# A hybrid encoder trunk: the order of the first unit's projections and the low-rank one in the second token half

## The chip, the cores and the metric

The kernel runs on one core of a Trainium2 chip. The metric is device time in microseconds, from launch to end, as the median of several runs. Beside it there is one execution with the hardware profiler on, whose trace is read here.

The engines are named as the profile names them: PE is TensorE's matrix multiply and PEld its weight load, DVE is VectorE, ACT is ScalarE, POOL is GpSimd, SP is SyncE, on which nearly all transfers are issued. [...]

## The reference

Two layers over 1024 tokens of width 1024. The change is in layer 0, in front of two groups of heads:

```python
h = rmsnorm(x, norm_mix_g[i])
proj = h @ even_w_in[e]                      # r, k, v of RWKV; q, k, v, gate of DeltaNet
dh = token_shift(h) - h
...
r = r + (token_shift(r) - r) * mu_proj[0]    # and so k, v
xw = h + dh * mu_lora[0]
xa = h + dh * mu_lora[1]
xg = h + dh * mu_lora[2]
w_log = -jax.nn.softplus(-(w0 + jnp.tanh(xw @ w1) @ w2).astype(jnp.float32)) - 0.5
decay = jnp.exp(-jnp.exp(w_log))
a = jax.nn.sigmoid(a0 + (xa @ a1) @ a2)
g = jax.nn.sigmoid(xg @ g1) @ g2
...
y = wkv7_scan(rh, heads(decay), kh, vh, -kk, kk * ah)
```

RWKV-7 has eight heads of 64 with a state that is carried from token to token, DeltaNet four heads of 128 in chunks. Their outputs are joined and projected; a squared-ReLU MLP and a gated embedding follow, and layer 1 has banded attention in place of the two groups.

## The kernel before

Activations lie with the feature on the partitions. Every 32-bit product is made of three: weights and activations are split in a rounded high part and a rest (`split_w`, L276 on ACT and L277 on DVE, for weights; `split_scaled`, L320 on ACT and L321 on DVE, for activations), and `mm3` does high times high, high times low and low times high. A projection of one 128-wide output over 512 tokens is so 24 matmuls of 128x512 into one PSUM bank (tag `dense`, name `dps`; there are two such banks in this layer), and is then scaled by the row norm `self.rs` and written out by a DVE instruction (L640 in `project`, L665 for the first part of the low-rank product). The row norm is made of sums of squares: `row_stats` (matmuls with ones, then a reciprocal root of small DVE instructions, L259 to L264) and `to_rows` (four transposes into a bank, a copy on ACT, L354). Both take their bank from the same two.

Layer 0 runs over 16 units: four RWKV pairs of heads and four DeltaNet heads, by turns, for the first 512 tokens (units 0 to 7), and then the same for the other 512 (8 to 15). Six generators ("lanes") emit the work: `in` makes a unit's projections, `front`, `mid`, `back` and `post` its scan, and one makes the cumulated decays. `run` steps through them by an estimated time: a lane gives a key for which it waits, or a name with a delay from a table. `rwkv_in` waits for `("raw", u - 2, j)` ahead of its projection j: for unit 8, until `front` of unit 6 has read its own. The order in which the lanes emit is only a preference: a planner (`schedule_with_timeline_sim=True`) then lays down the order on each engine, by its own picture of when things are ready and when a buffer is free, so loads are often issued far ahead of where they stand in the text.

Buffers that matter here:
- `wraw`, two of 128x1024: raw weights, two of the four tiles of x for the second half, the low-rank weight as it is loaded (`lraw`), its two scaled versions, and `sb`, the second low-rank product.
- `whi` and `wlo`, two each: the split weights, held until their projection is done.
- `xg` (pool `rx`): x of the current half, scaled and split. It can be written for the second half only behind the last matmul of the first that reads it.
- `gate`, two: the gate projection of a DeltaNet unit, held until `gdn_post` has read it (L1160).

`l0_in` is the lane of projections. At unit 8 it does, in this order: four loads of x, eight splits into `xg`, the low-rank product "la" (`lora(0, ...)`), then `rwkv_in` with three projections j = 1, 0, 2, each with a weight load and a split of its own; then `gdn_scalars` (a projection `wba` and a long chain of small DVE instructions) and the other low-rank product "lg". `lora` loads one weight (L651), makes two scaled versions of it on POOL (L659), splits both, runs two projections and adds the results on POOL (L668). At unit 0 the order is already another one: the first weight tile is loaded ahead of x (`self.w_first`), and the three projections come before la.

POOL also runs the substitution of the 16x16 inverses for `front` (`inverse_start`, L376 to L386), whose data go out and back through DRAM (`scr<-N`, `scr<-Ng` L364; `subb` L368; `z` L388; `Xp` L390), issued on SP.

Of the kernel before, what the change touches and what calls it, by code (L numbers as in the profile page):

```python
# [104 lines left out]
class Trunk:  # L105
# [423 lines left out]
    def l0_in(self, units):  # L529
        nc, a, fr = self.nc, self.a, self.fr  # L530
        self.state = {}
        self.xg = []
        for u, (nm, p, hf) in enumerate(units):
            if u % 8 == 0:


                self.xg, squares = [], []
                if hf == 0:
                    acc = fr.tile([P, HB], F32, tag="rsbc", name="acc", bufs=2)
                    self.w_first = self.load_w(a["w_in"][4])  # L540
                else:

                    x2 = [self.load_x(q, self.pre if q < 2 else self.wp, "ph" if q == 0 else "pl" if q == 1 else "wraw")
                          for q in range(4)]
                for k in range(NK):
                    if hf == 0:
                        xr = self.t2()
                        nc.sync.dma_start(out=xr, in_=a["x"][k, :, 0:HB])
                    else:
                        xr = x2[k // 2][:, k % 2, :]  # L550
                    if k % 2 == 0:
                        xg2 = self.pair(k // 2)
                    xg = xg2[:, k % 2]
                    self.split_scaled(xg, xr, self.vec("mixg", k), slice(0, HB))
                    self.xg.append(xg)
                    if hf == 0:
                        squares.append(lambda k=k, xr=xr: self.square(acc, xr, k == 0))
                for f in squares:
                    f()
                if hf == 0:  # L560
                    self.wa2 = fr.tile([P, 512], F32, tag="wa2", name="wa2")
                    nc.sync.dma_start(out=self.wa2, in_=a["wa2"])
                    self.g2 = self.l0.tile([P, 512], F32, tag="g2", name="g2")
                    nc.sync.dma_start(out=self.g2, in_=a["g2"])
                    self.hv = self.l0.tile([P, 2, 4], F32, tag="hv", name="hv")
                    nc.sync.dma_start(out=self.hv.rearrange("p a b -> p (a b)"),
                                      in_=a["gdnhv"].rearrange("(o c) -> o c", o=1).broadcast_to((P, 8)))
                    self.ea = self.l0.tile([P, 1, 4], F32, tag="ea", name="ea")
                    nc.scalar.activation(self.ea, self.hv[:, 0:1, :], AF.Exp)
                sc = {}  # L570
                if hf == 0:
                    rsc = self.sm.tile([P, 4], F32, tag="rsc", name="rsc")
                    self.rs = fr.tile([P, HB], F32, tag="rsbc", name="rsbc", bufs=2)

                    self.extra = [lambda t=t: self.psm.tile([P, HB], F32, tag=t, name="dps") for t in ("y", "ch", "pm")]
                    self.late, self.plan = [], {2: lambda: self.row_stats([acc], rsc), 3: lambda: self.to_rows(rsc, self.rs)}
                    raws = yield from getattr(self, nm + "_in")(p, hf, u)
                else:
                    self.rs = acc
                self.pst = None  # L580
                sc["lwa"] = yield from self.lora(0, [(0, 64, 0), (64, 128, 1)], "la")
                nc.scalar.activation(sc["lwa"][0:64], sc["lwa"][0:64], AF.Tanh)
            if u:
                raws = yield from getattr(self, nm + "_in")(p, hf, u)
            self.state[u] = (raws, sc)
            self.mark(("in", u), 1.0)
            if u == 6:

                acc = fr.tile([P, HB], F32, tag="rsbc", name="acc", bufs=2)
                for q in range(4):  # L590
                    x2 = self.load_x(q, self.pre, "pl" if q % 2 else "ph")
                    for e in range(2):
                        self.square(acc, x2[:, e], q + e == 0)
            if u == 7:
                rsc = self.sm.tile([P, 4], F32, tag="rsc", name="rsc")
                self.row_stats([acc], rsc)
                yield "l0_in1"
                self.to_rows(rsc, acc)
            if u % 8 == 0:

                yield from self.gdn_scalars(hf, sc)
                gg = yield from self.lora(1, [(0, 128, 2)], "lg")
                nc.scalar.activation(gg, gg, AF.Tanh, scale=0.5)
                nc.vector.tensor_scalar(gg, gg, 0.5, 0.5, op0=ALU.mult, op1=ALU.add)
                sc["lg"] = gg
                self.mark(("lg", hf))

        rsb = lambda: fr.tile([P, HB], F32, tag="rsbc", name="xs", bufs=2)
        pt = [self.pair(k) for k in range(2)]
        sc = [self.pair(q, F32) for q in (2, 3)]  # L610
        sc = [t[:, e] for t in sc for e in range(2)]
        yield from self.ple_proj(0, lambda k, hf: pt[k][:, hf], sc[0], lambda n: sc[1 + n % 3], rsb, self.load_w)
        yield from self.out_early(0, a["x"], self.pair, rsb, self.load_w, [("post", 7), ("post", 13), ("post", 14), ("post", 15)])
# [127 lines left out]
    def rwkv_in(self, p, hf, u):  # L741
        raws = []
        for j in (1, 0, 2):
            if u >= 2:
                yield ("raw", u - 2, j)
            w = self.load_w(self.a["w_in"][4 * j + p]) if u or j != 1 else self.w_first
            raws.append((yield from self.project(w, f"r{p}{j}", 1)))
        return [raws[1], raws[0], raws[2]]

# [1219 lines left out]
```

## Time and profile before

| | us |
|---|---|
| median of 3 runs | 3195.7 |
| lowest and highest run | 3192.25, 3198.93 |
| span of the profiled execution | 3188.9 |
| PE busy | 3080.8 (97%) |
| PEld busy | 2580.6 (81%) |
| DVE busy | 2005.1 (63%) |
| ACT busy | 1405.7 (44%) |
| POOL busy | 531.1 (17%) |

The span reaches from the first to the last instruction of the profiled execution; the median of the runs is 6.8 us above it. Busy time of PE is not work at full speed: the ends of matmuls are modelled, and TensorE's clock can be granted in part, which the profile shows as a share of full speed. Units 0 to 7 are projected from 7 to 346 us of the span, units 8 to 15 from 363 on; layer 0's mixer is over at about 960.

### The profile page before, as it was taken

To read this page: it belongs to the slowest core of one execution; us is meant where nothing else is said; L and a number is where in the kernel's file an instruction comes from. 1 tells how busy PE (TensorE), PEld (TensorE's weight loads), DVE (VectorE), ACT (ScalarE), POOL (GpSimd) and SP (SyncE) were. 2 spreads that over 40 slices of the span, in tenths; PEclk is the share of its full clock that TensorE was granted. 3 is DMA by queue.
4 is the path that set the end of the run, shared out by engine and by line. 5 is a ranking of instruction groups with operands and counts; after the bars stand their busy time and mean duration, and the time that the engine had idled before them with its cause. 6 is when DMAs were issued, how large, how long until landed. Compare 5 with 4: busy or idle time off the path is not lost.

```text
span 3188.9 us, 45834 instructions
## 1 busy us (share of the span) xinstructions
PE 3080.8 (97%) x17448; PEld 2580.6 (81%) x17448; DVE 2005.1 (63%) x4020; ACT 1405.7 (44%) x2640; POOL 531.1 (17%) x982
## 2 busy tenths in 40 slices
PE   7999999999999999999999899989999999999999
PEld 5887778877877888888888888888878888888887
DVE  6565675557748766655546576776768666655552
ACT  4343443334426555312123477777756554312121
POOL 6334443434500000000004210110200000000002
PEclk8999889999899999999999999999999999999999
DMA  3312112222336433523213210110256333522313
GB/s 121 94 60 63 47 40 71 64 62 78 119 107 200 148 122 109 189 94 105 93 53 126 70 36 32 48 39 16 76 177 215 139 119 109 190 100 93 106 47 106
DMA packets 144715, 309.58 MB, mean 97 GB/s; under 512 B 40944, under 2 KB 43120, under 8 KB 144496
## 3 DMA queue, kind: packets, MB, share of 16 engines
q1 hardware_dynamic: 126064, 273.10, 25.8%
q10 hardware_dynamic: 18432, 33.56, 2.7%
q8 instruction: 137, 2.24, 0.3%
q14 instruction: 82, 0.67, 0.1%
HBM read 232.16 MB, written 74.45 MB: 96 GB/s over the span
## 4 chain that ended last, share of the span: by engine, by line
PE 86%; DVE 8%; ACT 4%; DMA 1%; issue 1%; POOL 0%; SPq 0%; DVEq 0%; ACTq 0%
PE dps L161 71%; PE ch L161 2%; PE iz L161 2%; PE tp L161 1%; PE po L161 1%; PE pm L161 1%; PE py L161 1%; PE pt L165 1%; DVE ptile L318 1%; PE sn L161 1%; PE pp L161 1%; DVE pb L1809 1%; ACT pb L1822 1%; DMA wraw<-in_w_qkv 1%; PE sc L161 1%
## 5 line engine op out<-in xcount | busy, mean ns | idle before, releaser
L161 PE MATMUL dps<-r,act 128*128 128x512 f32 x3528 | 824.3, 392 | 0.0
L161 PEld LDWEIGHTS dps<-r,act 128*128 128x128 f32 x3528 | 662.1, 188 | 145.7
L161 PE MATMUL dps<-xg,whi 128*128 128x512 f32 x1280 | 435.1, 416 | 12.7 <-ACT xg L320 7.2
L161 PE MATMUL dps<-late,act 128*128 128x512 f32 x1536 | 352.9, 391 | 0.0
L161 PEld LDWEIGHTS dps<-late,act 128*128 128x128 f32 x1536 | 288.5, 188 | 63.1
L161 PE MATMUL dps<-wq,act 128*128 128x384 f32 x1536 | 304.5, 344 | 6.9 <-DVE vs L1718 3.5
L1466 POOL TENSOR_TENSOR pn<-pn,prs 128x512 f32<-128x512 f32 x32 | 45.2, 1415 | 1587.7 <-ACT prs L354 1492.5
L161 PEld LDWEIGHTS dps<-xg,whi 128*128 128x128 f32 x1280 | 245.1, 196 | 67.6 <-ACT xg L320 7.2
L161 PEld LDWEIGHTS dps<-wq,act 128*128 128x128 f32 x1536 | 265.5, 191 | 11.1 <-DVE vs L1718 5.5
L161 PE MATMUL dps<-xg,wlo 128*128 128x512 f32 x640 | 264.5, 414 | 1.5 <-DVE wlo L277 1.5
L1342 DVE TENSOR_TENSOR late<-late,dps 128x512 f32<-128x512 f32 x224 | 152.9, 685 | 150.9 <-PE dps L161 120.2
L1441 DVE TENSOR_TENSOR xw<-xw,dps 128x512 f32<-128x512 f32 x192 | 131.6, 686 | 148.5 <-PE dps L161 147.5
L1240 ACT CAST act<-act 128x1024 fp32r<-128x1024 f32 (+1 forms) x99 | 94.7, 963 | 284.9 <-DMA act<-in_w 158.2
L1240 ACT CAST act<-late 128x512 fp32r<-128x512 f32 x210 | 124.6, 618 | 140.5 <-PE dps L161 121.3
L1241 DVE TENSOR_TENSOR act<-late,act 128x512 fp32r<-128x512 f32 x210 | 139.9, 688 | 27.2 <-ACT act L1240 26.9
L161 PEld LDWEIGHTS dps<-xg,wlo 128*128 128x128 f32 x640 | 125.6, 196 | 28.0 <-DVE wlo L277 2.8
L161 PE MATMUL dps<-xw,act 128*128 128x512 f32 x576 | 138.9, 392 | 0.0
L276 ACT CAST whi<-wraw 128x1024 fp32r<-128x1024 f32 x78 | 81.6, 1046 | 120.6 <-PE dps L161 81.6
L161 PEld LDWEIGHTS dps<-xw,act 128*128 128x128 f32 x576 | 108.1, 188 | 24.1
L1241 DVE TENSOR_TENSOR act<-act 128x1024 fp32r<-128x1024 f32 (+1 forms) x99 | 109.9, 1115 | 20.8 <-ACT act L1240 20.1
L277 DVE TENSOR_TENSOR wlo<-wraw,whi 128x1024 fp32r<-128x1024 f32 x78 | 99.3, 1274 | 36.5 <-ACT whi L276 35.7
L161 PE MATMUL po<-ptile,vs 128*128 128x256 f32 (+1 forms) x576 | 103.7, 292 | 15.5 <-ACT ptile L317 7.1
(474 smaller groups left out, 5410.7 us busy)
## 6 DMA issues: line engine op xcount, KB each, us to landing
act<-in_w SPq DMA_DIRECT2D x68, 512.0 KB
hd<-late ACTq DMA_DIRECT2D x128, 256.0 KB
late<-in_w SPq DMA_DIRECT2D x60, 512.0 KB
wraw<-in_w_in SPq DMA_DIRECT2D x56, 512.0 KB
act<-hd SPq DMA_DIRECT2D x56, 512.0 KB
wraw<-in_w_out SPq DMA_DIRECT2D x21, 512.0 KB
wraw<-in_w_qkv SPq DMA_DIRECT2D x21, 512.0 KB
pn<-pnd SPq DMA_DIRECT2D x32, 256.0 KB
```

Of the source, the lines that this page charges most:

```text
L161: return self.nc.tensor.matmul(out, lhsT, rhs, start=start, stop=stop)
L165: return self.nc.tensor.transpose(out, in_, ident)
L276: nc.scalar.copy(hi, raw)
L277: nc.vector.tensor_tensor(lo, raw, hi.bitcast(F32), op=ALU.subtract)
L318: nc.vector.tensor_tensor(dst[:, 1, sl], src, dst[:, 0, sl].bitcast(F32), op=ALU.subtract)
L1240: A.copy(hi, s)
L1241: V.tensor_tensor(lo, s, hi.bitcast(F32), op=ALU.subtract)
L1342: V.tensor_tensor(r, t, u, op=ALU.add)
L1441: V.tensor_tensor(x[n][:, sl], x[n][:, sl], ps, op=ALU.add)
L1466: G.tensor_tensor(pn, pn, prs[:, sl], op=ALU.mult)
L1809: V.tensor_tensor_reduce(S, pn[:, 0:nn * P], toep[:, (3 - nn) * P:], op0=ALU.add, op1=ALU.max, scale=1.0, scalar=NEG, accum_out=mx[:, 0:1])
L1822: A.activation(S, S, AF.Exp, bias=mx[:, 2:3], accum_out=l[:, 0:1])
```

## The change

At unit 8, too, the first weight tile (`a["w_in"][4]`, the one of j = 1) is loaded and split ahead of the loads of x, the three projections of `rwkv_in` are emitted before the low-rank product la, and `rwkv_in` takes the tile that is already there. Nothing else is edited; which engine does what, the sizes and the number of instructions stay.

```diff
                 self.xg, squares = [], []
                 if hf == 0:
                     acc = fr.tile([P, HB], F32, tag="rsbc", name="acc", bufs=2)
-                    self.w_first = self.load_w(a["w_in"][4])
-                else:
-
+                self.w_first = self.load_w(a["w_in"][4])
+                if hf:
                     x2 = [self.load_x(q, self.pre if q < 2 else self.wp, "ph" if q == 0 else "pl" if q == 1 else "wraw")
                           for q in range(4)]
...
                     self.late, self.plan = [], {2: lambda: self.row_stats([acc], rsc), 3: lambda: self.to_rows(rsc, self.rs)}
-                    raws = yield from getattr(self, nm + "_in")(p, hf, u)
                 else:
                     self.rs = acc
+                raws = yield from getattr(self, nm + "_in")(p, hf, u)
                 self.pst = None
                 sc["lwa"] = yield from self.lora(0, [(0, 64, 0), (64, 128, 1)], "la")
                 nc.scalar.activation(sc["lwa"][0:64], sc["lwa"][0:64], AF.Tanh)
-            if u:
+            else:
                 raws = yield from getattr(self, nm + "_in")(p, hf, u)
...
-            w = self.load_w(self.a["w_in"][4 * j + p]) if u or j != 1 else self.w_first
+            w = self.load_w(self.a["w_in"][4 * j + p]) if u % 8 or j != 1 else self.w_first
```

## The prediction

> **What bounds the kernel now.** I read the page first, then the stretches of the place that is changed, then the order of events there on each engine.
>
> ```profile
> span 3188.9 us, 45834 instructions
> PE 86%; DVE 8%; ACT 4%; DMA 1%; issue 1%; POOL 0%; SPq 0%; DVEq 0%; ACTq 0%
> PEclk8999889999899999999999999999999999999999
> ```
> The chain that ended last is TensorE for 86% of the span: what counts is TensorE time. Whatever leaves TensorE idle, or at a low clock, is lost. The clock row has its 8s early, in the layer that is edited. The stretches around the handover from the first token half to the second (start:end, length, then busy time of PE, PEld, DVE, ACT and POOL, granted clock, DMA share, GB/s):
>
> ```profile
> 346.20:355.00 8.80, 6.83 (x51) 4.86 (x49) 7.70 (x24) 4.06 (x8) 5.57 (x11) 0.96 0.21 68
> 355.00:363.40 8.40, 8.32 (x71) 7.37 (x71) 6.54 (x14) 5.92 (x11) 5.83 (x7) 0.50 0.01 2
> 363.40:370.00 6.60, 6.60 (x23) 5.25 (x21) 6.10 (x8) 2.69 (x6) 1.92 (x3) 0.65 0.24 79
> 346.20:371.30 25.10, 23.05 (x151) 18.71 (x149) 20.34 (x43) 12.66 (x23) 13.32 (x20) 0.73 0.14 46
> ```
> TensorE is hardly idle here but is granted half its clock. Lost at the handover: idle 1.97 + 0.08, then 0.04 × 6.83 = 0.27, 0.50 × 8.32 = 4.16 and 0.35 × 6.60 = 2.31 to the clock, together **8.8 us**. That is all that this place has to give. The timeline of TensorE tells why (start, duration, engine, line, operation, count, idle before it):
>
> ```profile
> 346.19 0.95 PE L161 MATMUL dps<-ones,acc 128*128 128x1 f32 x8
> 355.05 0.80 PE L161 MATMUL ch<-Sg,KQ 128*128 128x128 f32 x2 [2.02 <-DVE Sg L1128]
> 358.92 1.12 PE L165 MATMUL dps<-ident,rsc 128*128 128x128 f32 x4
> 363.39 1.22 PE L161 MATMUL dps<-xg,whi 128*128 128x512 f32 x2
> ```
> The last projection of the first half ends where the row sums (`dps<-ones,acc`) begin, at 346.2; the first one of the second half, the low-rank "la", starts at 363.39. For 17.2 us TensorE has only the scans' small matmuls. Why it is so late:
>
> ```profile
> 292.21 11.07 SPq L618 DMA_DIRECT2D xr<-in_x  x2
> 344.93 0.36 SPq L651 DMA_DIRECT2D lraw<-in_lora  x1
> ```
> ```profile
> 349.81 2.03 POOL L659 TENSOR_TENSOR wraw<-lraw,d_omul 128x512 f32<-128x512 f32 x2
> 356.36 2.49 POOL L659 TENSOR_TENSOR wraw<-lraw,vecs 128x512 f32<-128x512 f32 x2 [2.24 <-DVE rsw L263]
> ```
> ```profile
> 360.08 0.59 ACT L354 COPY acc<-dps 128x512 f32<-128x512 f32 x1 [0.72 <-PE dps L165]
> 339.53 4.07 ACT L320 ACTIVATE xg<-xr,vecs 128x512 fp32r<-128x512 f32 x6
> 346.39 1.33 ACT L320 ACTIVATE xg<-xr,vecs 128x512 fp32r<-128x512 f32 x2 [1.18 <-PE dps L161]
> ```
> The two `wraw` buffers hold x from 292 and 303 on until x is split (339.5 to 347.7), so the low-rank weight loads at 344.93 and then needs POOL and a split. But a second gate ends later: there are two `dps` banks. One is used by `to_rows` until 360.08 + 0.59 = 360.67; the other is held by the last gate projection (u = 7):
>
> ```profile
> 333.88 0.69 DVE L640 TENSOR_TENSOR raw<-dps,rsbc 128x512 f32<-128x512 f32 x1 [0.66 <-PE dps L161]
> 349.50 2.62 DVE L787 TENSOR_SCALAR f<-f 128x512 f32<-128x512 f32 x1
> 366.95 0.68 DVE L1160 SCALAR_TENSOR_TENSOR o<-o,gate 128x512 f32<-128x512 f32 x1
> 368.82 0.68 DVE L640 TENSOR_TENSOR gate<-dps,rsbc 128x512 f32<-128x512 f32 x1
> ```
> The gate's matmuls are over at 346.2, but its result leaves the bank only at 368.82 to 369.50, because its `gate` buffer (two of them) is read by an earlier unit's `post` until 366.95 + 0.68 = 367.63. **That bank is the point of this prediction: no edit touches it.**
>
> **The change part by part.** No instruction, byte or matmul is added: the same weight tile is loaded once, earlier.
>
> *First weight tile ahead of x.* `w_first` takes the `wraw` buffer that x's third load has now (292.21), x's third load takes the next, and the fourth waits for the split of `w_first`. That split needs the weight buffers of the projection that is evacuated at 333.88, so it starts near 334.
>
> ```profile
> 375.75 1.06 ACT L276 CAST whi<-wraw 128x1024 fp32r<-128x1024 f32 x1 [1.31 <-issue]
> 376.83 1.23 DVE L277 TENSOR_TENSOR wlo<-wraw,whi 128x1024 fp32r<-128x1024 f32 x1 [0.20 <-ACT whi L276]
> 310.17 3.87 PE dps L161 x17
> ```
> A split is 1.06 + 1.23 = 2.3 us, and a load takes at most 349.81 − 344.93 = 4.9 us: x's last quarter is there at about 341.3, and its splits cannot start before 346.39 anyway. Cost nothing, with 5 us to spare; if that cover were gone, each microsecond would delay the first projection by one. On SP the fourth x load can stand in front of other issues while it waits, as x's pair does now for 11.07 us; what comes behind it there feeds inverses that are used tens of microseconds later. I take 0.
>
> *Projections first.* The first of them needs x, `w_first` and a bank, all there at about 347, so its 24 matmuls run in the gap: by 3.87 / 17 = 0.228 us each (a row of the chain), 5.5 us. Then dense work stops again. It sits in the bank that `to_rows` used, and cannot leave before `acc` is made; `to_rows` now has to wait for the gate's bank, 369.50, plus its own 360.67 − 358.92 = 1.75 us. The second projection starts near **371.3**. The stretch without dense work is 351.7 to 371.3 instead of 346.2 to 363.4: 19.6 us, not 17.2.
>
> The sum over 346.2 to 371.3: TensorE did 23.05 × 0.73 = 16.8 us of full-clock work, of which 21 matmuls of la (4.8 us), so 12.0 us of scan. Afterwards it does 5.5 + 12.0 = 17.5: **−0.7 us**. The scans reach the gate's release at another time, too: POOL's scaling (349.81 to 351.84) leaves this place, and the DVE instruction beside it is short again.
>
> ```profile
> L787 DVE TENSOR_SCALAR f<-f x8: 415/427/2625, 50.4 to 779.1; 128x512 f32<-128x512 f32 x8
> ```
> Over all its eight instances this line takes 415/427/2625 ns (least, median, most): 2.62 us here against 0.43, and the chain runs through it into the 2.02 us for which TensorE waits: **−2.2 us**. Against that, 5.5 us of matmuls now stand in front of the scan's: +5.5, less what a full clock would give back from 355 to 363.4, 0.50 × 8.32 = 4.2: **+1.3 us**. Together **−1.6 us**. Bounds: all that is lost comes back, −8.8; the clock stays where it was, −0.7 − 2.2 + 5.5 = +2.6. I take −1.6, nearest to the rows of the gap itself.
>
> [...]
>
> *Low-rank projection third.* Its load, two scalings and two splits now lie beside the second and third projection. Between la's first result and the fifth projection's are four intervals:
>
> ```profile
> 375.94 0.69 DVE L665 TENSOR_TENSOR lao<-dps,acc 128x512 f32<-128x512 f32 x1 [0.23 <-PE dps L161]
> 417.90 0.69 DVE L640 TENSOR_TENSOR raw<-dps,acc 128x512 f32<-128x512 f32 x1
> 442.35 1.12 PE L161 MATMUL tp<-lao,wa 64*128 64x512 f32 x2
> ```
> (417.90 − 375.94) / 4 = 10.5 us each, so 21 us cover about 4.9 + 2.0 + 2.3 us of preparing. Its two products are evacuated near 371.3 + 3 × 10.5 = 403 and 413; the first reader of the result (`tp<-lao,wa`) comes at 442.35. Cost 0; the price if the cover fails is the rival on the slow side. The fifth projection ends about when it does now (417.90), so `wba` and the second low-rank one, "lg", keep their places: 0.
>
> Forecast: 3188.9 − 1.6 = 3187.3 of span. The median of the runs is 3195.7, which is 6.8 above the span: **3194.1 us**. It passes to the end in full, since TensorE is busy to the last with dense work after it:
>
> ```profile
> 890.00:940.00 50.00, 50.00 (x365) 41.06 (x364) 24.76 (x52) 14.79 (x26) 1.14 (x4) 0.97 0.37 122
> ```
>
> **Rivals.** *The gap closes.* If the planner frees the gate's bank early, all 8.8 us come back: 3186.9. Against it: the order of 366.95 and 368.82. 0.12.
>
> *lg gains by the shift.* lg has a hole of its own:
>
> ```profile
> 433.61 0.33 SPq L364 DMA_DIRECT2D scr<-Ng  x1
> 437.15 0.36 SPq L651 DMA_DIRECT2D lraw<-in_lora  x1
> ```
> ```profile
> 440.00:450.00 10.00, 9.05 (x73) 6.42 (x71) 8.61 (x25) 4.94 (x13) 5.84 (x14) 1.00 0.08 30
> 450.00:460.00 10.00, 7.18 (x50) 5.89 (x48) 9.79 (x22) 4.61 (x7) 6.86 (x13) 1.00 0.04 6
> 460.00:470.00 10.00, 7.96 (x35) 7.25 (x35) 9.52 (x26) 4.82 (x11) 7.51 (x12) 0.51 0.20 62
> ```
> Its load is issued behind another on SP. Lost: idle 0.95 + 2.82 + 2.04 and 0.49 × 7.96 = 3.9 to the clock, 9.7 us. If the new order lets that load pass, or the small DVE work of `gdn_scalars` leaves this stretch (DVE is 98% busy), the forecast loses 9.7 more: 3184.4. 0.20.
>
> *la starves in its new place (slower).* POOL runs the next inverse's chain in one piece:
>
> ```profile
> 391.42 0.50 POOL L376 TENSOR_SCALAR_AFFINE_SELECT sub<-subb 64x256 f32<-64x256 f32 x1 [1.58 <-DMA subb<-scr]
> 403.60 0.65 POOL L386 COPY sub<-sub 64x256 f32<-64x256 f32 x1
> ```
> If la's scaling is not issued before 391.42, it comes after 404.25 and la's weight is ready at 404.25 + 2.0 + 2.3 = 408.6, while the third projection ends at 371.3 + 2 × 10.5 = 392.3: 16.3 us without dense work. At the gap's own rate, 8.8 / 17.2 = 0.51, that is 8.3 us; lg's hole costs 9.7. With 9: 3203.1. It decides at POOL's 391.42. 0.19.
>
> *The clock does not return.* The scans alone leave too many holes and the half clock lasts as now: +2.6, 3198.3. For it: half clock was granted in a stretch that was 99% busy, after only 1.97 us idle. 0.12. [...]
>
> *It does nothing:* the planner keeps the order on TensorE, 3195.7. 0.05. The forecast keeps 0.32.
>
> **How the numbers follow.** About 0.2%, 6.4 us, is what can be told from no change here: faster is below 3189.3, slower above 3202.1. Faster: 0.12 + 0.20 = 0.32. Slower: 0.19. Same: 0.32 + 0.12 + 0.05 = 0.49. The range reaches to the lg case (3184.4) and the slow one (3203.1), with 2 to 3 us beyond each, as each price is off by that much: 3182 to 3206.
>
> **What would show it.** Right: on TensorE a projection from about 347 to 353 at full clock, none until `to_rows`' transposes near 370; L787 near 0.43; x's fourth load issued near 336; la's evacuations near 403 and 413. Wrong: dense work between 355 and 368 (the bank was free); la's scaling behind POOL's inverse chain; lg's load ahead of `scr<-Ng`; TensorE idle or at half clock after 440 in other amounts than now.

## The result and the profile after

| | median, us | lowest, highest | runs |
|---|---|---|---|
| before | 3196.55 | 3191.20, 3207.01 | 20 |
| after | 3191.47 | 3186.08, 3198.03 | 20 |

After divided by before is 0.9984, with a 95% interval of 0.9977 to 0.9992: 5.1 us less by the medians, 2.6 to 7.4 by the interval. By the medians that is inside the prediction's bound of 0.2% (6.4 us); the far end of the interval is not. One execution alone cannot show such a difference, since the runs of one kernel are 12 to 16 us apart; the profiled execution of after even has a span 1.2 us longer than that of before. What follows therefore compares places, and not spans.

The page of after, in the lines that answer to those of before (span, chain that ended last, granted clock in 40 slices):

```profile
span 3190.1 us, 45833 instructions
PE 85%; DVE 8%; ACT 4%; DMA 2%; issue 1%; POOL 0%; SPq 0%; DVEq 0%; ACTq 0%
PEclk8999999999899999999999999999999999999999
```

TensorE still sets the end, and of the four 8s of before two are left. The same stretches of the handover in after (start:end, length, busy time of PE, PEld, DVE, ACT, POOL, granted clock, DMA share, GB/s):

```profile
346.20:355.00 8.80, 8.68 (x59) 6.30 (x60) 6.73 (x20) 4.79 (x8) 5.19 (x13) 1.00 0.52 167
355.00:363.40 8.40, 7.70 (x82) 6.43 (x83) 6.33 (x20) 6.74 (x15) 4.30 (x5) 1.00 0.11 30
363.40:370.00 6.60, 6.60 (x58) 5.83 (x56) 6.22 (x18) 1.81 (x6) 1.99 (x3) 0.93 0.01 2
370.00:380.00 10.00, 10.00 (x68) 7.91 (x68) 4.70 (x11) 1.31 (x2) 4.28 (x7) 0.70 0.00 1
```

Loss is idle time plus the busy time that the clock takes away. Here that is 0.12 + 0.70, then 0.07 × 6.60 = 0.46 and 0.30 × 10.00 = 3.0, together 4.3 us, where before lost 8.8. Of the 1.97 us idle in the first stretch 0.12 are left, 0.70 have come up in the second, and a shorter piece of low clock has moved behind 363. The timelines of after, by engine (start, duration, engine, line, operation, count, idle before it and its releaser):

```profile
347.77 0.95 PE L161 MATMUL dps<-ones,acc 128*128 128x1 f32 x8
357.24 0.60 PE L165 MATMUL dps<-ident,rsc 128*128 128x128 f32 x4
360.53 0.74 PE L161 MATMUL dps<-xg,whi 128*128 128x512 f32 x2
...
371.95 1.05 PE L161 MATMUL dps<-xg,whi 128*128 128x512 f32 x2
...
352.26 0.41 DVE L786 TENSOR_SCALAR f<-f 128x512 f32<-128x512 f32 x1
367.14 0.68 DVE L639 TENSOR_TENSOR gate<-dps,rsbc 128x512 f32<-128x512 f32 x1
378.20 0.69 DVE L1160 TENSOR_TENSOR o<-o,pp 128x512 f32<-128x512 f32 x1 [4.13 <-PE pp L165]
...
374.15 2.04 POOL L658 TENSOR_TENSOR wraw<-lraw,d_omul 128x512 f32<-128x512 f32 x2
385.89 2.04 POOL L658 TENSOR_TENSOR wraw<-lraw,vecs 128x512 f32<-128x512 f32 x2 [1.30 <-DVE wlo L277]
389.44 0.50 POOL L376 TENSOR_SCALAR_AFFINE_SELECT sub<-subb 64x256 f32<-64x256 f32 x1 [1.25 <-DMA subb<-scr]
```

The first projection of the second half starts at 360.53, behind the transposes of `to_rows` (357.24), and not at 347; the second one starts at 371.95. la's scaling has left the gap: the first one stands at 374.15, where DVE waits for TensorE anyway (4.13 us ahead of 378.20).

Some 90 us later lies lg's hole, which is there as before. The stretch and its reason in after:

```profile
450.00:460.00 10.00, 4.89 (x30) 4.05 (x28) 9.90 (x20) 4.99 (x9) 8.63 (x15) 0.89 0.15 52
460.00:470.00 10.00, 10.00 (x35) 8.58 (x35) 5.40 (x23) 2.00 (x9) 1.55 (x3) 0.50 0.22 67
```
```profile
429.83 0.34 SPq L364 DMA_DIRECT2D scr<-Ng  x1
433.44 0.36 SPq L650 DMA_DIRECT2D lraw<-in_lora  x1
...
443.12 2.18 DVE L786 TENSOR_SCALAR f<-f 128x512 f32<-128x512 f32 x1
451.56 2.90 DVE L705 TENSOR_TENSOR gs_poly<-gs_poly,gs_s 128x16 f32<-128x16 f32 x1
...
451.74 1.26 POOL L822 TENSOR_TENSOR f<-f 128x512 f32<-128x512 f32 x1
...
456.33 0.49 PE L161 MATMUL ch<-W,F 128*128 128x128 f32 x2 [3.00 <-DVE W L1116]
```

DVE is 99% busy with `gdn_scalars` and the scan of the first unit at once, one of its small products takes 2.90 us beside POOL's work, and TensorE waits. From 450 to 470 that costs 5.11 idle, 0.11 × 4.89 and 0.50 × 10.00: 10.6 us.

### The profile page after: what moved, and what is told of

It reads as the page before. It is cut to its first block, busy times and chain, and to the rows that moved or that the text cites. A ratio compares the mean times of both kernels' runs of the same rounds, so it can differ in the third digit from the quotient of the medians.

```text
span 3190.1 us, 45833 instructions
## 1 busy us (share of the span) xinstructions
PE 3082.4 (97%) x17448; PEld 2584.5 (81%) x17448; DVE 2006.6 (63%) x4020; ACT 1403.5 (44%) x2640; POOL 535.2 (17%) x982
## 4 chain that ended last, share of the span: by engine, by line
PE 85%; DVE 8%; ACT 4%; DMA 2%; issue 1%; POOL 0%; SPq 0%; DVEq 0%; ACTq 0%
PE dps L161 70%; PE ch L161 2%; PE iz L161 2%; PE tp L161 1%; PE po L161 1%; PE pm L161 1%; PE py L161 1%; PE pt L165 1%; DMA wraw<-in_w_qkv 1%; DVE ptile L318 1%; PE sn L161 1%; PE pp L161 1%; DVE pb L1808 1%; DVE wq L1676 0%; ACT pb L1821 0%
## 5 line engine op out<-in xcount | busy, mean ns | idle before, releaser
L161 PE MATMUL dps<-xg,whi 128*128 128x512 f32 x1280 | 437.5, 418 | 12.8 <-ACT xg L320 7.6
L161 PE MATMUL po<-ptile,vs 128*128 128x256 f32 (+1 forms) x576 | 105.8, 296 | 17.6 <-ACT ptile L317 8.4
```

What stands on the lines that cost most here:

```text
L161: return self.nc.tensor.matmul(out, lhsT, rhs, start=start, stop=stop)
```

## The experiments

Three theories stood at the outset; "dense" is a matmul of a projection or of a low-rank product. **A**: no dense matmul of the second half can start before `to_rows`, whatever the weight does; what helps is the order, which takes la's scaling out of the gap. **B**: the weight that is ready early is what helps. **C**: any edit makes the planner fall into another order over the next hundreds of us, and the gain is that luck.

### The two parts apart

e1 has the order of the change without the early weight; e2 the early weight without the order.

```diff
 e1, against before
-                    raws = yield from getattr(self, nm + "_in")(p, hf, u)
                 else:
                     self.rs = acc
+                raws = yield from getattr(self, nm + "_in")(p, hf, u)
...
-            if u:
+            else:
                 raws = yield from getattr(self, nm + "_in")(p, hf, u)
 e2, against before
-                    self.w_first = self.load_w(a["w_in"][4])
-                else:
+                self.w_first = self.load_w(a["w_in"][4])
+                if hf:
...
-            w = self.load_w(self.a["w_in"][4 * j + p]) if u or j != 1 else self.w_first
+            w = self.load_w(self.a["w_in"][4 * j + p]) if u % 8 or j != 1 else self.w_first
```

> The change without the early weight: at unit 8 the projections come before the low-rank product, but the first weight tile loads behind x. Theory A (the first dense matmul of the second half waits for to_rows, whatever its weight does; what helped is that the low-rank scaling on POOL left the gap): the same as the changed kernel, about 5 us under before; its weight is split near 352, to_rows near 357, first dense matmul near 360. Theory B (the weight that is ready early is what helped): the gain is gone, within 2 us of before. Theory C (the planner's reshuffling of everything behind gives a few us either way by chance): no relation to either.

> The other half of the change: the first weight tile loads ahead of x, but the low-rank product is still emitted first. Theory A: no gain, within 3 us of before; low-rank scaling on POOL still lies in the gap and the first dense matmul comes near 363 or later, as w_first now also takes one of the two split-weight buffers. Theory B: about 5 us under before. Theory C: no relation.

e1: 3194.02 beside 3197.47, ratio 0.9984 (0.9972 to 0.9995). e2: 3195.32, ratio 0.9994 (0.9986 to 1.0003). By the ratios the order alone gives what the whole change gives, and the early weight alone gives nothing that can be told. That speaks against B as the main cause; it does not exclude it, since the two intervals overlap. In e1 the first dense matmul of the second half starts at 364.98, right behind the transposes again, as A says, but 5 us later than A expected. The traces do not bear out A's gain at the handover: from 346.2 to 380 e1 loses 8.0 us and e2 8.5, nearly what before lost. The queue of SP in e1 shows another thing:

```profile
424.94 0.36 SPq L651 DMA_DIRECT2D lraw<-in_lora  x1
438.52 0.33 SPq L364 DMA_DIRECT2D scr<-Ng  x1
```

Here lg's load does pass `scr<-Ng`, and lg's hole is gone (TensorE is busy 19.87 of the 20 us from 450 to 470, at clock 1.00). Yet the median is not 10 us better. The profiled execution is one of the fastest three of eleven (3183.1 to 3187.2; the other eight lie from 3192.1 to 3199.4); what those lose has not been seen. So e1 has the ratio of the whole change, but not its trace, and the equal ratios do not show that the two gain in the same place.

### The bank

e7 is after, but `row_stats` and `to_rows` take a bank of the scans (`tp`) at unit 7, so that nothing stands between the first projection and the dense bank.

```diff
+                self.pst = self.psm
                 self.row_stats([acc], rsc)
                 yield "l0_in1"
                 self.to_rows(rsc, acc)
+                self.pst = None
```

> The kernel after, but at unit 7 row_stats and to_rows take their PSUM bank from the scans' pool (tag tp) instead of the two dense banks, so that nothing is asked of the dense banks between the last gate projection and the first projection of the second half. Theory A (the prediction failed because the dense bank was promised to to_rows, which was emitted first): the first projection of the second half starts by about 350 instead of 360.5, runs in the gap, TensorE at half clock after 363 lasts less than the 6 us of the kernel after, and the second projection still waits for the gate's bank or for the row norm, near 366 to 371; the median is 2 to 5 us below that of the kernel after, 3186 to 3190 beside 3196.5. Rival R1 (the first projection waits for x or for its weight, not for a bank): it still starts at about 360, and the median is that of the kernel after, 3190 to 3193. Rival R2 (the scans pay for the bank): the row sums or the rows of unit 7 hold a tp bank that the fronts need, new idle time of TensorE between 340 and 365, the median above that of the kernel after.

3215.06 beside 3196.97, ratio 1.0054 (1.0040 to 1.0068). TensorE in e7:

```profile
347.23 0.62 PE L161 MATMUL dps<-xg,whi 128*128 128x512 f32 x2
...
378.78 1.22 PE L161 MATMUL dps<-xg,whi 128*128 128x512 f32 x2
...
395.88 0.95 PE L161 MATMUL st<-ones,acc 128*128 128x1 f32 x8
...
402.34 0.62 PE L165 MATMUL st<-ident,rsc 128*128 128x128 f32 x4 [0.79 <-DVE f L1015]
```

The first projection now starts at 347.23, straight behind the last gate projection: x and the weight had been there, so it was the bank that held it until 360.5 in after. Rival R1 falls. But R2 holds too, and far beyond what was expected (the forecast was 3186 to 3190): in the queue for a `tp` bank the row sums come up only at 395.88, 48 us later than in after. Without the row norm nothing of the second half can be evacuated; the first projection keeps its bank until 404, the gate's projection keeps the other until 373, and TensorE has no dense work between 356.0 and 378.8. One wait was taken away and a longer one put in its place.

### The row norm earlier

If the bank is held because the rows are late, they can be made sooner: e5 (on after) and e6 (on before) do `row_stats` and `to_rows` behind unit 6, right after the squares they are made of. That is one line less.

```diff
-            if u == 7:
                 rsc = self.sm.tile([P, 4], F32, tag="rsc", name="rsc")
                 self.row_stats([acc], rsc)
                 yield "l0_in1"
                 self.to_rows(rsc, acc)
```

> The changed kernel with the second half's row norm (row_stats and to_rows) emitted behind unit 6 in place of unit 7, so that it is done before the gap. Theory A: the first dense matmul starts near 347, right behind the last gate projection, as w_first and x are there; the stretch without dense work is gone, and the 4 us of idle and half clock that the changed kernel still has there come back: 3 to 5 us under the changed kernel, 8 to 10 under before. Rival (the gate projection's bank is the limit, as the prediction had it): the first projection starts near 347, but the next one waits until near 368, gain over the changed kernel under 2 us.

> The kernel before with the row norm emitted behind unit 6. Theory A with two gates in a row (to_rows, and behind it the low-rank weight, ready at 356.3): the first dense matmul comes near 356 to 357, 7 us earlier than before, and 2 to 4 us are gained. If the low-rank weight alone was the gate: first dense matmul stays near 363, nothing gained.

e5: 3184.14, ratio 0.9959 (0.9946 to 0.9972). e6: 3179.99, ratio 0.9939 (0.9926 to 0.9953), both beside 3197.47. The direction was expected. The size is larger: for e6 17 us where 2 to 4 were forecast, for e5 some 8 below after where 3 to 5 were. And it did not come the way that was expected. e6 by stretches at the same times, around the old handover and lg's place:

```profile
346.20:355.00 8.80, 8.80 (x45) 6.14 (x44) 6.03 (x10) 3.46 (x7) 7.70 (x19) 1.00 0.31 95
355.00:363.40 8.40, 8.40 (x60) 6.52 (x59) 5.78 (x14) 5.03 (x9) 7.28 (x18) 1.00 0.18 63
363.40:370.00 6.60, 5.37 (x64) 4.35 (x63) 6.07 (x9) 3.11 (x6) 5.31 (x6) 1.00 0.11 20
370.00:380.00 10.00, 9.68 (x82) 7.94 (x82) 6.11 (x22) 4.54 (x13) 4.52 (x7) 0.91 0.31 90
...
450.00:460.00 10.00, 10.00 (x63) 7.60 (x63) 5.17 (x10) 4.55 (x9) 8.29 (x23) 1.00 0.39 125
460.00:470.00 10.00, 10.00 (x58) 7.48 (x58) 7.45 (x14) 5.39 (x10) 6.16 (x12) 1.00 0.25 75
```

From 346.2 to 380 e6 loses 1.23 + 0.32 + 0.09 × 9.68 = 2.4 us instead of 8.8, and lg's hole is shut. But the handover itself is no longer there. TensorE in e6 between the last matmul of the first half and the first of the second:

```profile
332.15 0.39 PE L161 MATMUL dps<-xg,wlo 128*128 128x512 f32 x1
344.02 0.71 PE L161 MATMUL dps<-xg,whi 128*128 128x512 f32 x2
```

With the row norm asked for earlier, the first half is projected earlier too: it ends at 332.5 instead of 346.3, the second half begins at 344.0 (356 to 357 was expected), and the stretch without dense work is 11.5 us instead of 17.2, at full clock. Around the row norm's new place there is another such stretch, from 282.7 to 293.9; before had one from 300.5 to 309.9. Why lg's hole shuts is in SP's queue and on DVE, in e6 and, last line, in before:

```profile
404.02 0.53 SPq L650 DMA_DIRECT2D lraw<-in_lora  x1
441.67 0.33 SPq L364 DMA_DIRECT2D scr<-Ng  x1
...
414.11 0.67 DVE L676 TENSOR_TENSOR ba<-dps,acc 8x512 f32<-8x512 f32 x1
...
436.44 0.68 DVE L677 TENSOR_TENSOR ba<-dps,acc 8x512 f32<-8x512 f32 x1 [0.44 <-PE dps L161]
```

`wba` is evacuated at 414.11 (before: 436.44), so the chain of `gdn_scalars` and lg's load (404.02, before 437.15) come ahead of `scr<-Ng` and of the scan that they collided with. The same holds in every trace: where lg's load is ahead of `scr<-Ng` (e1 and all runs with early rows) TensorE loses at most 1.5 us from 440 to 480, where it is behind (before, after, e2, e7, e10, e11, e15) 7.9 to 14.4.

In e5 the handover does not close. Its first projection is made ahead of 346.5, its second one up to 358.0, and then there is no dense work for 15.7 us:

```profile
357.63 0.39 PE L161 MATMUL dps<-xg,wlo 128*128 128x512 f32 x1
373.75 1.22 PE L161 MATMUL dps<-xg,whi 128*128 128x512 f32 x2
...
373.00 0.69 DVE L638 TENSOR_TENSOR gate<-dps,rsbc 128x512 f32<-128x512 f32 x1
```

It ends when the gate's projection of unit 7 leaves its bank: this is the wait that the prediction called its point. e5 loses 5.0 us from 346.2 to 380, no less than after, so theory A's forecast that the stretch would be gone is a miss, and the rival's mechanism is what the trace shows, though not its small gain.

Two more complete the square: order alone with early rows (e9) and early weight alone with early rows (e12).

> The order of the change without the early weight, and the row norm made behind unit 6 as in e5 and e6. e6 (low-rank product first) was 4 us faster than e5 (whole change). Theory W (the early weight is what costs that: it holds one of the two weight buffers from about 292 on): this run is near e6, 3178 to 3182 where the kernel before has 3197. Theory L (with the row norm out of the way the low-rank product is better placed first): this run is near e5, 3182 to 3187. Theory C (the rest is the planner's reshuffling): it falls anywhere in 3176 to 3190, and the windows from 330 to 480 do not order the three as their times do.

> The fourth corner with the row norm behind unit 6: the weight tile ahead of x, the low-rank product first. So far: neither part 3180.0 (e6), whole change 3184.1 (e5), order alone 3185.6 (e9). Theory L (with the rows out of the way the low-rank product is better first, since its two products fill the gap and projections first cost about 5): 3177 to 3183. Theory W (the early weight costs it): 3183 to 3188. Theory C (which order the planner falls into decides): outside both, or e6 run again leaves its own 3180 by more than 3.

e9: 3185.56 beside 3196.97, ratio 0.9964 (0.9950 to 0.9978). e12: 3175.21 beside 3198.11, ratio 0.9933 (0.9915 to 0.9952). All eight cells as ratios to before:

| | rows behind unit 7 | rows behind unit 6 |
|---|---|---|
| low-rank first | 1 | 0.9939 (e6), 0.9952 (e14, below) |
| low-rank first, weight early | 0.9994 (e2) | 0.9933 (e12) |
| projections first | 0.9984 (e1) | 0.9964 (e9) |
| projections first, weight early | 0.9984 (after), 0.9989 (e10, below) | 0.9959 (e5) |

The early weight brings or costs nothing that can be told in any pair, so nothing supports theory W. L is favoured, as e9 is near e5 and e12 near e6; e12's 3175.2 lies below L's range of 3177 to 3183, which the expectation left to theory C, but its six runs spread over 18 us. From 330 to 480 TensorE loses 10.6 us in e6, 13.6 in e5 and 20.3 in e9, in the order of their times, which speaks against C. Projections first is a little better as long as the rows are late, and on the whole worse by some 0.2% once they are in time, though the closest pair (e5, e14) differs by 0.07% only. Why la first is then better is in part to be seen: in e6 la's two products leave their bank at 358.08 and 369.92, and dense work follows each, while in e5 both banks are full from 358.0 to 373.7. No run tests it.

e13 makes the row norm behind unit 5, squares and loads with it; e14 is e6 again.

```diff
 e13, against e6
-            if u == 6:
+            if u == 5:
```

> The kernel before with the row norm of the second half made behind unit 5 instead of 6, squares and loads with it. If the rows' lateness is all that stood between the two halves, e6 already has that gain, and one unit more of lead brings nothing: within 2 us of e6. Rival: the loads and squares collide with unit 6's work, or hold the second row buffer and the scans' buffers longer, slower than e6 by over 3 us.

> e6 once more (the kernel before with the row norm behind unit 6), beside the two others on one chip: 3177 to 3183 where the kernel before has 3197, ratio 0.993 to 0.9955. Theory C, that e6 had good luck in its order, would show only in another program, not here; a median over 3186 would say that e6's five rounds were too few.

e13: 3177.42, ratio 0.9944 (0.9928 to 0.9960); e14: 3179.58, ratio 0.9952 (0.9938 to 0.9966), both beside 3198.11. More lead brings nothing that can be told, and e6 repeats. So before with the rows behind unit 6 is faster than both kernels, by about 18 us of the one and, by the ratios, 10 to 16 of the other; with the early weight on top (e12) it is at least as fast.

### How much is chance

e10 is the changed kernel again. e11 alters one number of the lanes' estimate from unit 8 on; by the names in the trace the order on TensorE stays that of after until about 516 us, far behind the handover and lg's place, and differs behind it. e15 is before again.

```diff
 e11, against after
-            self.mark(("in", u), 1.0)
+            self.mark(("in", u), 0.5 if u >= 8 else 1.0)
```

> The changed kernel itself once more, beside the others on one chip. The order of instructions is the same, so the first projection starts again only behind the rows, at 360 plus or minus 3, and its median is 3 to 7 us under that of the kernel before. The theory that the stretch 440 to 480 (idle 5.1 us and half clock in the first trace) belongs to the planned order: TensorE is idle again for 4 to 6 us there and at half clock behind it. The rival, that it depends on the execution: another amount, by over 2 us.

> The changed kernel with one number in the estimate of the lanes edited from unit 8 on (0.5 instead of 1.0 as the delay behind a finished unit's projections). Nothing is computed otherwise; the planned order on TensorE is that of the kernel after up to the sixth projection of the second half and differs behind it. Theory A (the gain is made at the handover): it keeps the gain, within 2 us of the change run beside it. Theory C (a reshuffled order behind the handover is worth as much as the change): it differs from the change by 3 us or more, either way.

> The kernel before once more, for a second trace. Three traces with the changed handover's order of TensorE (the change, e10, e11) lost 4.3, 0.7 and 8.5 us between 346.2 and 380, by idle time and clock; before lost 8.8 in its one trace. Theory P (the half clock there follows the execution, not the order): before loses another amount this time, by over 2 us, with the same idle of about 2.0 us ahead of the scan at 355 and the same 2.6 us on L787. Theory O (the order sets it): 7.5 to 10 again.

e10: 3192.97 beside 3196.97, ratio 0.9989 (0.9980 to 0.9999). e11: 3195.95 beside the same, ratio 0.9998 (0.9988 to 1.0008). e15: 3201.29 beside 3198.41, ratio 1.0010 (0.9995 to 1.0025). An edit that leaves the handover's order alone moves the median by 3.0 us. That is the size that C asked for, but it is not clear of noise, since the intervals of e10 and e11 overlap; e11 can't be told from before, and it can't be told from e10 either. C is not excluded. The handover in e10, order unchanged:

```profile
363.40:370.00 6.60, 6.60 (x73) 5.76 (x72) 6.07 (x21) 1.41 (x5) 1.30 (x3) 1.00 0.01 2
370.00:380.00 10.00, 10.00 (x69) 8.27 (x68) 4.88 (x10) 2.45 (x6) 4.39 (x7) 1.00 0.20 79
```

and in e11:

```profile
355.00:363.40 8.40, 8.38 (x50) 7.16 (x49) 3.56 (x16) 3.77 (x9) 1.18 (x3) 0.50 0.29 80
363.40:370.00 6.60, 6.60 (x53) 5.62 (x54) 5.13 (x9) 4.06 (x8) 3.90 (x4) 0.57 0.00 0
```

e10 never falls to half clock there and loses 0.7 us, all of it idle time (0.12 + 0.60); e11 loses 8.5 us from 346.2 to 380, all but 0.02 to the clock (1.5 ahead of 355, then 0.50 × 8.38 and 0.43 × 6.60); the first trace of after lost 4.3. With the clock the stretch without dense work changes too: 12.8 us in after, 12.6 in e10, 18.0 in e11 (348.6 to 366.64), on one order. Before lost 8.8 and, in e15, 7.4 (idle 1.65 + 1.05, to the clock 0.37 × 7.35 and 0.30 × 6.60). That is between what theories P and O asked for: with before's order a low clock came in both traces, with after's order the loss was anything from 0.7 to 8.5. lg's hole, in contrast, comes back in e10: TensorE is idle 3.02, 0.46 and 1.17 us at the same three matmuls, 3.00, 0.46 and 1.65 in the first trace. **The larger idle times go with the planned order; how long the low clock lasts differs from execution to execution.** Nor does little idle time go with a full clock: e11 and e2, granted 0.50 to 0.57 from 355 to 370, are idle for 0.02 and 0.01 us from 346.2 to 380.

Summed in the same way over longer stretches, in steps of 5 and 10 us, TensorE's losses are:

| us | before, e15 | after, e10, e11 | e6, e14 |
|---|---|---|---|
| 330 to 480 | 25.5, 26.4 | 17.6, 13.8, 21.7 | 10.6, 6.8 |
| 480 to 3160 | 104.5, 111.9 | 115.2, 117.0, 117.3 | 114.2, 109.1 |

By these traces the change saves some 8 us around the place that is edited and loses about as much behind it, where before's two traces alone differ by 7 us. Which of it makes the 5 us of the medians is not shown. Early rows save some 17 us at the place, which is the size of their gain.

e15 also bears on the term of DVE and POOL. All engines in e15, the rows that count:

```profile
349.82 0.43 DVE L787 TENSOR_SCALAR f<-f 128x512 f32<-128x512 f32 x1
...
351.59 2.50 DVE L262 TENSOR_TENSOR rsw<-rsc 128x4 f32<-128x4 f32 x1
...
351.44 0.62 POOL L386 COPY sub<-sub 32x256 f32<-32x256 f32 x1
352.03 2.03 POOL L659 TENSOR_TENSOR wraw<-lraw,d_omul 128x512 f32<-128x512 f32 x2
...
355.41 0.49 PE L161 MATMUL ch<-Sg,KQ 128*128 128x128 f32 x2 [2.06 <-DVE Sg L1128]
```

POOL comes 2.2 us later than in the first trace of before, L787 is short (0.43 us), and another instruction is long: a product of four elements a row that takes 0.15 us a moment later takes 2.50, and ends as POOL's does (354.09 and 354.06). A POOL copy (351.44) was already running when it began, and the scaling followed that without a break. The first trace of before has the same copy ahead of its scaling:

```profile
349.21 0.63 POOL L386 COPY sub<-sub 32x256 f32<-32x256 f32 x1
```

It was running when L787 began at 349.50, the scaling followed at 349.81, and L787 and the scaling end at 352.12 and 351.84. TensorE waits 2.06 us in e15, as it did for 2.02. So the wait is not bound to L787: in both traces the long instruction begins beside POOL's copy and ends within 0.3 us of the scaling behind it. Why it lasts so long is not shown. What the place costs differs: in e2, where la is still first, the four scans of L790 on DVE take 3.75 us from 355.82 (1.38 in e15), and TensorE, at a clock of 0.55 from 355 to 363.4, is idle there for 0.01 us.

## Why the prediction was right, and where it was not

The time is 3191.5 where 3194.1 was forecast: faster than before by 5.1 us, not by 1.6, and inside the 0.2%. That the number is so near is in good part luck. The range, 3182 to 3206, has before itself in it; of the three terms of the −1.6 two did not take place; and the span, forecast at 3187.3, was 3190.1. The 6.8 us that the sum puts between span and median are mostly scatter: in every later run the time is 1.7 to 2.5 us above its own span, so the trace of before was one of a quick execution.

- *What bounds*: right. TensorE is 85% of the chain, and what the handover and lg's hole lose is idle time and clock.
- *First weight tile ahead of x, cost 0*: right. x's fourth load was issued at 337.11 (forecast: near 336), and e2 shows neither gain nor loss that can be told.
- *Projections first*: **the step that failed** is "The first of them needs x, `w_first` and a bank, all there at about 347, so its 24 matmuls run in the gap". It started at 360.53. The bank was free but asked for earlier by `to_rows`, which is emitted first; here the bank went to the request that was emitted first, not to the one that was ready. e7 shows that nothing else was missing (347.23). The gate's bank, "the point of this prediction", came free at 367.14 + 0.68 = 367.82 (forecast: 369.50), and the second projection started at 371.95 (forecast: 371.3). That agreement is luck: the bank had been free for 4 us, and the second projection waited for the first one to end. The gate's bank does set the pace in e5, once the rows are early.
- *The terms −0.7 and +1.3*: both were worked out for the projection in the gap, and neither took place. That such a projection brings the full clock back was the author's estimate: from 355 to 363.4 the clock was 0.91 in e7, where a projection runs from 347.23, and 1.00, 1.00 and 0.50 in after, e10 and e11, where none starts before 360. Instead the stretch without dense work went from 17.2 to about 12.8 us (347.77 to 360.53): it began 1.6 us later, the rows came sooner (their transposes at 357.24 instead of 358.92), and the first projection 3.3 us behind them instead of 4.5. In e11, on the same order, it was 18.0 us.
- *The term −2.2*: right in place and size for the handover. TensorE's idle time from 346.2 to 355 went from 1.97 to 0.12 us, and DVE's long instruction is gone there. Which instruction is the long one changes: L787 in the trace of before (2.62 us), another in e15 (2.50). Beside la's scaling in its new place none is long: at 374.15 DVE waits for TensorE, and its instructions beside 385.89 take 0.55 and 0.68 us. But L786, 0.41 us long at the handover now, takes 2.18 at 443.12 beside lg's scaling, and 2.18 again at 439.77 in e10 (0.51 in before). TensorE is busy then; whether it deepens lg's hole, for which DVE is late, is not shown.
- *Low-rank third, cost 0*: right. Its scalings, at 374.15 and 385.89, pass ahead of POOL's inverse chain (389.44), the second by only 389.44 − 385.89 − 2.04 = 1.5 us: the slow rival was as close as that. Its second product came at 423.46, 10 us behind the forecast 413, still ahead of its first reader at 440.56.
- *lg*: its load stayed behind `scr<-Ng`, as the forecast assumed. What the rival names, the load that passes, came about in e1, without the gain in the median, and in e6.
- *The clock*: forecast as one number, it is a spread. By the traces the handover lost 8.8 and 7.4 with before's order, 4.3, 0.7 and 8.5 with after's: on the mean 8.1 and 4.5. But the three with the change lie 7.8 us apart, so these 3.6 us between the means are not shown to be the change's, and e1 lost 8.0 there. That the kernel is faster by some 5 us is measured twice (5.1, and 4.0 in e10); where it gains them stays open.

## What to carry to other kernels

Before work is put into a gap, ask which buffer it will take and who asked for that buffer earlier: in e7 and after, work that was ready did not pass a request that was emitted before (the first projection at 360.53 in after, the row sums at 395.88 in e7). Then look at what that earlier request waits for: here it was the row norm, and taking out one line, which makes it sooner, was worth some three times the change. A difference of a few us in a planned kernel needs the same kernel traced more than once and one harmless edit beside it, and even then a trace may not show where it is made.

## What was not expected of the hardware

- One planned order, three executions (after, e10, e11), and from 363.4 to 370 the granted clock was 0.93, 1.00 and 0.57. The idle time in these stretches does not foretell it: e11 had 0.02 us of it from 346.2 to 380, the least of the three, and the lowest clock. Why the three differ, and why a stretch that the profile shows as fully busy (6.60 of 6.60 us in e11) was granted 0.57, is not shown.
- A DVE product on 128x4 elements took 2.50 us (e15, 351.59) and one on 128x16 took 2.90 (after, 451.56), 0.15 to 0.27 otherwise in these stretches, beside POOL instructions that follow one another without a break.
